# The order of the loads between an attention's end and the first half of an output projection

## Chip, core and metric

The kernel runs on one core of a Trainium2 chip. The metric is device time in microseconds (us) of one execution; lower is better. The engines are PE (TensorE, matrix products), ACT (ScalarE), DVE (VectorE), POOL (GpSimd) and SP (SyncE, which here issues every load and store). Each works through its own list of instructions in order and waits on semaphores for the others.

## The reference

One layer of a hybrid encoder on 1024 tokens of width 1024, with 16 meta tokens ahead of them, all in float32:

```python
h = concat([meta_tokens, x])                 # 1040 rows
u = rmsnorm(h, norm_mix)
a, q, k, v, r, lr, ga, gb = split(u @ w_in)
y_a = (multiscale_pool(a) grouped @ w_pool_mix * pool_scale) @ w_pool_out
o = chunked_gated_linear_attention(q, k, v, log_decay(lr @ w_gate_up + b_gate))   # chunks of 64
y_b = (rmsnorm(o, gla_norm) * silu(r)) @ w_gla_out
m = sigmoid(ga) * y_a + sigmoid(gb) * y_b
h = h + m @ w_out
h = h + square(relu(rmsnorm(h, norm_ffn) @ w_ff1)) @ w_ff2
out = rmsnorm(h, norm_final) without the meta rows
```

The change lies around `y_b`, `m` and `m @ w_out`.

## The kernel before

Float32 products are made of three fp32r matmuls (`mm3`): each operand is split into a high part (ACT copies it to fp32r) and a low part (the rest, a subtraction on DVE, or on POOL while the attention runs). So a block of weights goes through a load into a raw tile, the high part on ACT and the low part on DVE or POOL before PE can use it.

The tokens are worked on in two halves of 512, called half 0 and half 1. The attention (`gla`) has four units, two for each half; while it runs, filler work is poured between its steps: the projections for k, v and the gate gb, and then `yb_block(n, 0)`, the product with w_gla_out for half 0. `yb_block(n, h)` makes two products of 128 output columns each: 12 matmuls into a bank (L1044 and L1045 on DVE multiply it by the stored gate gb and add the stored y_a part, ACT copies the high part th at L1048, POOL makes the low part tl at L1049). Half 0 and half 1 have eight such products each. The gate tiles come from HBM in pairs, a tile of gb_dram (L992) and one of ma_dram (L993), by `yb_load`, into three buffers for each half (t and o); a buffer is free when POOL has made the tl of the product that used it.

The weights of w_gla_out come in four blocks of 512 KB through a ring of two (`Ring`): `top_up` loads the next block into a raw tile (L101) and splits it (L77 on ACT, L78 on DVE or POOL) as soon as a place in the ring is counted as done. Half 0 uses blocks 0 to 3, and keeps 2 and 3; half 1 uses 2 and 3 from the ring first, then loads 0 and 1 again (`YB`).

The output projection follows. w_out is loaded and split in two column halves of four blocks each (`load_wo(ch, kk)`, L1324 and L1325), of 512 KB. `out_tile(t, ch)` makes 128 tokens by 512 columns with 24 matmuls, and DVE adds the bank to x (L1357), which `x_again(t)` has loaded again into the tile `acc`. `acc` (eight tiles of 512 KB) lies where the attention's buffers were, so its pool opens when the last user of those buffers is done.

What sets the order: PE's list is in program order throughout (`tc.manual_schedule`). The lists of ACT and DVE are in program order from `early_gates` to `wo1_open`. The list of SP is made by a scheduler, which moves a load ahead of others when its place is free. `early_gates` stands in the code where the attention's last unit has been issued, in the middle of half 0's products.

Of the kernel before, what the change touches and what calls it, by code (L numbers as in the profile page):

```python
# [15 lines left out]
P = 128  # L16
D = 1024
# [3 lines left out]
HALF = 512  # L21
# [84 lines left out]
def kernel(  # L106
# [3 lines left out]
    nc = tc.nc  # L110
# [3 lines left out]
    w_gate_up, b_gate, gla_norm, w_gla_out, w_out = w_gate_up[0], b_gate[0], gla_norm[0], w_gla_out[0], w_out[0]  # L114
    norm_ffn, w_ff1, w_ff2 = norm_ffn[0], w_ff1[0], w_ff2[0]
# [8 lines left out]
    def banks(keep=0, **tags):  # L124
        while len(ps_open) > keep:
            ps_open.pop().__exit__(None, None, None)
            wide.pop(psp.popitem()[0], None)
        for tag, n in tags.items():
            cm = tc.tile_pool(name=f"ps_{tag}", bufs=n, space=bass.MemoryType.PSUM)
            psp[tag] = cm.__enter__()  # L130
            ps_open.append(cm)
# [31 lines left out]
    gB = left.push("gB", [P, D], F32)  # L163
# [16 lines left out]
    raw = Raw(nc, [left.push(f"raw{i}", [P, D], F32) for i in range(2)])  # L180
# [10 lines left out]
    def f32(ap):  # L191
        return ap.bitcast(F32)
# [4 lines left out]
    def bcast(v):  # L197
        return v[None, :].broadcast_to([P, D])
# [202 lines left out]
    S, rings = {}, [W1]  # L401

    def step(steps, fn, ring=None, aps=()):
        steps.append((ring, list(aps), fn))
# [29 lines left out]
    def buffer(key, depth, size=HALF):  # L434
        S[key] = left.push(key, [P, depth, size], F32)
        S["n" + key], S["d" + key] = 0, depth

    def nxt(key):
        i = S["n" + key]
        S["n" + key] += 1  # L440
        return S[key][:, i % S["d" + key]]
# [345 lines left out]
    one = []  # L787
# [122 lines left out]
    def rows4(w, j):  # L910
        return w[:, j * 256 : (j + 1) * 256].rearrange("(k p) c -> p k c", p=P)
# [74 lines left out]
    def yb_load(n, h):  # L986

        if n >= 8 or (n, h) in staged:
            return
        d = 2 * YB[h][n // 2] + n % 2  # L990
        gl, ml = staged[n, h] = (nxt("t2"), nxt("o2")) if h else (nxt("t1"), nxt("o"))
        nc.sync.dma_start(gl, gb_dram[d, h])  # L992
        nc.sync.dma_start(ml, ma_dram[d, h])  # L993

    def in_order(on):


        if on:
            S["order"] = tc.manual_schedule(engines={mybir.EngineType.Activation, mybir.EngineType.DVE})
            S["order"].__enter__()  # L1000
        else:
            S.pop("order").__exit__(None, None, None)

    def early_gates():

        in_order(True)
        left.pop_to(S["left_n"])
        for key in ("t2", "o2"):
            S[key] = right.push(key, [P, 3, HALF], F32)
            S["n" + key], S["d" + key] = 0, 3  # L1010
        S["raw3"] = right.push("raw3", [P, D], F32)
        for n in range(3):
            yb_load(n, 1)

    kept = {}

    def yb_block(n, h):
        j = YB[h][n]

        def fn(*wbs):  # L1020
            if h == 0 and n > 1:
                kept[j] = wbs[0]
            wb = wbs[0] if wbs else kept[j]
            hi, lo = (t.rearrange("p (k c) -> p k c", k=4) for t in wb)
            assert h or ("o", 0) in done
            yg = S["yg"][h]
            for e in range(2):
                d, w = 2 * j + e, slice(e * P, (e + 1) * P)
                for m in range(2 + h):
                    yb_load(2 * n + e + m, h)  # L1030
                gl, ml = staged[2 * n + e, h]
                b = bank("mm")
                for k in range(4):
                    mm3(
                        b, 1, lambda i: (hi[:, k, w], lo[:, k, w]),
                        lambda i: (yg[:, 0, k], yg[:, 1, k]), first=k == 0, last=k == 3,
                    )
                    yield 3 * 512 / 2400
                if e and not wbs:
                    W1.done, W1.kept = W1.done + 1, W1.kept - 1  # L1040
                    W1.top_up()
                elif e:
                    yield "keep" if j in kept else "free"
                dve.tensor_tensor(gl, b, gl, ALU.mult)  # L1044
                dve.tensor_tensor(gl, gl, ml, ALU.add)  # L1045
                th = MH[h][:, d]
                tl = ML[h][:, d]
                act.activation(th, gl, ACT.Copy)  # L1048
                pool.tensor_tensor(tl, gl, f32(th), ALU.subtract)  # L1049

        return fn
# [211 lines left out]
    def gla():  # L1263
# [16 lines left out]
        for n, u in enumerate(units + [None]):  # L1280
            if u is None:
                early_gates()
            live = side + old + ([inside(*u, units[n - 1] if n else None)] if u else [])
            while live:
                waits = [(g, next(g, None)) for g in live]
                live = [g for g, w in waits if w is not None]
                pour(max([w for _, w in waits if w is not None], default=0) * PACE)
                if not live:
                    break
            if n == 2:  # L1290
                done.add(("o", 0))
            if n == 0:
                while ("k", 1) not in done:
                    next(filler)
            old = [across(*u)] if u else []
            side = [meta_state(1)] if n == 0 else []
# [7 lines left out]
    def merge_open():  # L1304
        W1.eng = dve
        banks(keep=1, x=2, ms=4)
        rota["mm"] = ("mm", "mm", "x", "x")
        left.pop_to(base)
        S["wo"] = [left.push("wo0", [P, 2, KT, HALF], F32R)]
        S["left_acc"] = left.mark()  # L1310
        S["acc"] = left.push("acc", [P, 8, D], F32)
        raw.lend(S["raw3"])
        nc.sync.dma_start(gB, bcast(norm_ffn))

    def x_again(t):
        nc.sync.dma_start(S["acc"][:, t], x[t * P : (t + 1) * P, :])

    def load_wo(ch, kk):
        def fn():
            wo = S["wo"][ch][:, :, 2 * kk : 2 * kk + 2]  # L1320
            c = slice(ch * HALF, (ch + 1) * HALF)
            r = raw.load(w_out[kk * 256 : (kk + 1) * 256, c].rearrange("(k p) c -> p k c", p=P), D)
            r = r.rearrange("p (k c) -> p k c", k=2)
            act.activation(wo[:, 0], r, ACT.Copy)  # L1324
            dve.tensor_tensor(wo[:, 1], r, f32(wo[:, 0]), ALU.subtract)  # L1325

        return fn

    step(one, merge_open)
    def wo1_open():  # L1330
        in_order(False)
        raw.back()
        right.pop_to(0)
        buffer("u2", 2, D)
        S["u2p"] = right.push("u2p", [P, 2, HALF], F32)
        S["rawx0"] = right.push("rawx0", [P, D], F32)
        raw.lend(S["rawx0"])
        S["right_ff"] = right.mark()
        S["wo"].append(right.push("wo1", [P, 2, KT, HALF], F32R))
# [4 lines left out]
    def out_tile(t, ch):  # L1344
        def fn():
            half, at = t // 4, (t % 4) * P
            wo = S["wo"][ch]
            b, n = bank("mm"), ORDER.index(t)
            for j in range(2):
                if ch and j and n > 1:  # L1350
                    turn_tile(ORDER[n - 2])
                mm3(
                    b, KT // 2, lambda i: (MH[half][:, 4 * j + i, at : at + P], ML[half][:, 4 * j + i, at : at + P]),
                    lambda i: (wo[:, 0, 4 * j + i], wo[:, 1, 4 * j + i]), first=j == 0, last=j == 1,
                )
            a = S["acc"][:, t, ch * HALF : (ch + 1) * HALF]
            dve.tensor_tensor(a, b, a, ALU.add)  # L1357
            if ch:
                layer_norm(S["acc"][:, t], S["u2"][:, n % 2])
                nc.sync.dma_start(h_dram[t], S["acc"][:, t])  # L1360

        return fn
# [31 lines left out]
            dve.tensor_tensor(fl, a, f32(fh), ALU.subtract)  # L1394

    for n, j in enumerate(YB[1]):
        if n < 2:
            step(one, yb_block(n, 1))
        else:
            step(one, yb_block(n, 1), W1, [rows4(w_gla_out, j)])  # L1400
        if n:
            step(one, load_wo(0, n - 1))
    step(one, load_wo(0, 3))
    step(one, wo1_open)
    for t in range(8):
        step(one, lambda t=t: x_again(t))
        step(one, out_tile(t, 0))
        if 1 < t < 6:
            step(one, load_wo(1, t - 2))


    def first_blocks():
        ff_quarters.places = [raw.own, [S["rawx0"], None]]
        for i, u in ((0, 0), (0, 1), (1, 0)):
            ff_quarters.load(i, u)
# [262 lines left out]
```

## Time and profile before

| | us |
|---|---|
| three runs | 1247.72, 1245.71, 1245.96 |
| median | 1245.96 |
| span of the profiled execution | 1247.8 |

The page gives no time of the profiled execution beside its span; the span lies 0.1 us above the slowest of the three runs, so next to nothing lies around it.

| stretch of the profiled execution | from, us |
|---|---|
| first product with w_gla_out, half 0 | 466.0 |
| first output tile (m @ w_out) | 515.7 |
| second output tile | 531.4 |
| output tiles of w_out's second half end, squared-ReLU MLP follows | about 640 |

How to read it: PE is busy nearly throughout, so the places where PE waits are what a change in the order of loads can move. The views used below are the page, the waits of an engine, windows (busy time of each engine in a stretch, with the clock granted to PE and the share in which the DMA engines were busy) and the timeline of an engine. A row of a timeline has the start, the duration, the engine, the line, the operation, what is written and read, the count, and in brackets the idle time before it with what ended it.

### The profile page before, as it was taken

The numbers are of one execution on the slowest core, as the hardware profiler recorded it, in microseconds if no ns is written. First come the engines' busy times: TensorE is split into PE (matmuls) and PEld (weight loads), VectorE is DVE, ScalarE is ACT, GpSimd is POOL, SyncE is SP. The second block draws the span as 40 slices with busy tenths as digits, with TensorE's granted clock in tenths as the row PEclk, the third lists the DMA queues.
The fourth block names the chain that finished last, engine by engine and source line by source line (L and its number), as shares of the span: only waits on it lengthen the run. The fifth ranks groups of instructions, "written<-read, shape, count | busy, mean of one in ns | idle before, by whom it ended". The sixth has DMA issues, their size and how long they took to land.

```text
span 1247.8 us, 18255 instructions
## 1 busy us (share of the span) xinstructions
PE 1213.1 (97%) x6822; PEld 1006.5 (81%) x6822; DVE 850.7 (68%) x1384; ACT 615.4 (49%) x1092; POOL 65.0 (5%) x70
## 2 busy tenths in 40 slices
PE   7999999999999999799999999999999999999997
PEld 6878888988887788688878888888887788888886
DVE  6897676653556677723897676766774777887786
ACT  6667567321446663412654554555553444444554
POOL 2100000001101115300000000000000000000000
PEclk9999999999999999899999999999999999999999
DMA  8033326156102246831234544544569773333432
GB/s 249 2 109 104 109 85 197 52 161 204 36 19 61 86 140 223 284 104 51 94 117 155 167 152 136 164 156 135 177 219 371 267 247 94 102 93 100 162 96 90
DMA packets 142682, 173.85 MB, mean 139 GB/s; under 512 B 10969, under 2 KB 82417, under 8 KB 142593
## 3 DMA queue, kind: packets, MB, share of 16 engines
q1 hardware_dynamic: 142592, 172.68, 42.8%
q8 instruction: 54, 0.88, 0.3%
q14 instruction: 36, 0.29, 0.1%
HBM read 119.17 MB, written 53.48 MB: 138 GB/s over the span
## 4 chain that ended last, share of the span: by engine, by line
PE 90%; DVE 5%; DMA 2%; issue 1%; ACT 1%; SPq 0%; DVEq 0%; ACTq 0%
PE b_mm L246 11%; PE b_mm L247 11%; PE b_mm L248 11%; PE b_ms L246 9%; PE b_ms L247 9%; PE b_ms L248 9%; PE b_x L246 8%; PE b_x L248 8%; PE b_x L247 8%; PE b_sc L1128 1%; PE b_mx L246 1%; PE b_mx L247 1%; PE b_mx L248 1%; PE b_ms L538 1%; DMA raw<-hf_dram 1%
## 5 line engine op out<-in xcount | busy, mean ns | idle before, releaser
L246 PE MATMUL b_mm<-th,w1h 128*128 128x512 f32 (+1 forms) x312 | 117.8, 378 | 3.2 <-ACT th L1385 2.1
L247 PE MATMUL b_mm<-tl,w1h 128*128 128x512 f32 (+1 forms) x312 | 116.0, 372 | 0.6 <-DVE tl L1386 0.6
L248 PE MATMUL b_mm<-th,w1l 128*128 128x512 f32 (+1 forms) x312 | 115.8, 371 | 0.0
L246 PE MATMUL b_x<-th,w1h 128*128 128x512 f32 (+1 forms) x240 | 90.8, 378 | 0.0
L247 PE MATMUL b_x<-tl,w1h 128*128 128x512 f32 (+1 forms) x240 | 90.6, 378 | 0.0
L248 PE MATMUL b_x<-th,w1l 128*128 128x512 f32 (+1 forms) x240 | 90.3, 376 | 0.0
L264 ACT ACTIVATE w1h<-raw 128x512 fp32r<-128x512 f32 x96 | 59.6, 621 | 36.7 <-PE b_x L247 14.1
L265 DVE TENSOR_TENSOR w1l<-raw,w1h 128x512 fp32r<-128x512 f32 x96 | 65.6, 684 | 12.3 <-ACT w1h L264 12.3
L246 PEld LDWEIGHTS b_mm<-th,w1h 128*128 128x128 f32 x312 | 58.5, 188 | 16.5 <-issue 3.3
L264 ACT ACTIVATE w1h<-fs 128x512 fp32r<-128x512 f32 x72 | 45.4, 631 | 46.4 <-PE b_ms L247 31.7
L247 PEld LDWEIGHTS b_mm<-tl,w1h 128*128 128x128 f32 x312 | 58.6, 188 | 10.5 <-DVE tl L1386 0.9
L248 PEld LDWEIGHTS b_mm<-th,w1l 128*128 128x128 f32 x312 | 58.6, 188 | 10.3
L264 ACT ACTIVATE w1h<-bt 128x512 fp32r<-128x512 f32 x44 | 27.8, 632 | 67.7 <-issue 59.5
L265 DVE TENSOR_TENSOR w1l<-fs,w1h 128x512 fp32r<-128x512 f32 x72 | 49.3, 685 | 14.7 <-ACT w1h L264 14.6
L1535 DVE TENSOR_TENSOR bt<-w,w 128x512 f32<-128x512 f32 x80 | 54.6, 683 | 0.4 <-DMA w<-in_w_ff_dram 0.4
L248 PEld LDWEIGHTS b_x<-th,w1l 128*128 128x128 f32 x240 | 45.1, 188 | 8.5
L246 PEld LDWEIGHTS b_x<-th,w1h 128*128 128x128 f32 x240 | 45.0, 188 | 8.4
L247 PEld LDWEIGHTS b_x<-tl,w1h 128*128 128x128 f32 x240 | 45.1, 188 | 8.2
L264 ACT ACTIVATE fxh<-bt 128x512 fp32r<-128x512 f32 x36 | 22.8, 632 | 57.6 <-issue 48.1
L246 PE MATMUL b_ms<-wo,w1h 128*128 128x512 f32 x128 | 49.8, 389 | 0.0
L247 PE MATMUL b_ms<-wo,w1h 128*128 128x512 f32 x128 | 49.8, 389 | 0.0
L248 PE MATMUL b_ms<-wo,w1l 128*128 128x512 f32 x128 | 49.8, 389 | 0.0
(438 smaller groups left out, 3370.2 us busy)
## 6 DMA issues: line engine op xcount, KB each, us to landing
hf_dram<-h SPq DMA_DIRECT2D x112, 256.0 KB, 2.1
raw<-hf_dram SPq DMA_DIRECT2D x112, 256.0 KB, 2.6
w<-in_w_ff_dram SPq DMA_DIRECT2D x64, 256.0 KB, 4.8
raw<-in_w_in_dram SPq DMA_DIRECT2D x24, 512.0 KB, 4.8
raw<-in_w_ff_dram SPq DMA_DIRECT2D x16, 512.0 KB, 4.1
rawx<-in_w_ff_dram SPq DMA_DIRECT2D x16, 512.0 KB, 4.0
xs<-in_x_dram SPq DMA_DIRECT2D x8, 512.0 KB, 4.9
rawx<-in_w_in_dram SPq DMA_DIRECT2D x8, 512.0 KB, 4.4
```

Of the source, the lines that this page charges most:

```text
L246: pe.matmul(ps, ah, bh, start=first and i == 0, stop=False, skip_group_check=more)
L247: pe.matmul(ps, ah, bl, start=False, stop=False, skip_group_check=more)
L248: pe.matmul(ps, al, bh, start=False, stop=last and i == n - 1, skip_group_check=more)
L264: act.activation(hi, a, ACT.Copy)
L265: dve.tensor_tensor(lo, a, f32(hi), ALU.subtract)
L538: pe.transpose(b[j][:, i], u[:, (4 * j + i) * P : (4 * j + i + 1) * P], ident)
L1128: pe.matmul(b[to, e, j], kk[r, s], qq[r, s], start=True, stop=True, tile_position=(e * CH, u * CH))
L1535: dve.tensor_tensor(bt, w, S["w2"][q[3:]][:, i], ALU.add if q[2] == "+" else ALU.subtract)
```

## The change

- From `early_gates` to `first_blocks`, SP's list is in program order as well (`in_order` now takes a key and the engines).
- w_out's first half: block 0 is loaded in `early_gates` into the tile raw3, which took part in the rotation of raw tiles before; block 1 in `merge_open` into the idle tile `acc[:, 5]`; blocks 2 and 3 behind the first and the second `yb_block` of half 1, into `acc[:, 6]` and `acc[:, 7]`. The split of block n stands ahead of `yb_block(n, 1)` (before, that of block n - 1 stood behind it).
- norm_ffn (gB) is loaded behind half 1's products instead of in `merge_open`; x is loaded behind it, two tiles ahead of the output tiles.

```diff
-    def in_order(on):
-        if on:
-            S["order"] = tc.manual_schedule(engines={mybir.EngineType.Activation, mybir.EngineType.DVE})
-            S["order"].__enter__()
-        else:
-            S.pop("order").__exit__(None, None, None)
+    def in_order(key, *engines):
+        S[key] = tc.manual_schedule(engines=set(engines))
+        S[key].__enter__()
+
+    def any_order(key):
+        S.pop(key).__exit__(None, None, None)
 
     def early_gates():
-        in_order(True)
+        in_order("loads", mybir.EngineType.SP)
+        in_order("order", mybir.EngineType.Activation, mybir.EngineType.DVE)
...
         for n in range(3):
             yb_load(n, 1)
+        fetch_wo(0, 0, S["raw3"])
...
-        raw.lend(S["raw3"])
-        nc.sync.dma_start(gB, bcast(norm_ffn))
+        fetch_wo(0, 1, S["acc"][:, 5])
...
+    fetched = {}
+
+    def fetch_wo(ch, kk, at=None):
+        c, rows = slice(ch * HALF, (ch + 1) * HALF), w_out[kk * 256 : (kk + 1) * 256]
+        ap = rows[:, c].rearrange("(k p) c -> p k c", p=P)
+        if at is None:
+            at = raw.load(ap, D)
+        else:
+            nc.sync.dma_start(at.rearrange("p (k c) -> p k c", k=2), ap)
+        fetched[ch, kk] = at.rearrange("p (k c) -> p k c", k=2)
+
     def load_wo(ch, kk):
         def fn():
-            wo = S["wo"][ch][:, :, 2 * kk : 2 * kk + 2]
-            c = slice(ch * HALF, (ch + 1) * HALF)
-            r = raw.load(w_out[kk * 256 : (kk + 1) * 256, c].rearrange("(k p) c -> p k c", p=P), D)
-            r = r.rearrange("p (k c) -> p k c", k=2)
+            if (ch, kk) not in fetched:
+                fetch_wo(ch, kk)
+            wo, r = S["wo"][ch][:, :, 2 * kk : 2 * kk + 2], fetched.pop((ch, kk))
             act.activation(wo[:, 0], r, ACT.Copy)
             dve.tensor_tensor(wo[:, 1], r, f32(wo[:, 0]), ALU.subtract)
...
     for n, j in enumerate(YB[1]):
+        step(one, load_wo(0, n))
         if n < 2:
             step(one, yb_block(n, 1))
         else:
             step(one, yb_block(n, 1), W1, [rows4(w_gla_out, j)])
-        if n:
-            step(one, load_wo(0, n - 1))
-    step(one, load_wo(0, 3))
+        if n < 2:
+            step(one, lambda kk=n + 2: fetch_wo(0, kk, S["acc"][:, 4 + kk]))
+
+    def load_gB():
+        nc.sync.dma_start(gB, bcast(norm_ffn))
+
+    step(one, load_gB)
     step(one, wo1_open)
+    step(one, lambda: x_again(0))
+    step(one, lambda: x_again(1))
     for t in range(8):
-        step(one, lambda t=t: x_again(t))
+        if t < 6:
+            step(one, lambda t=t: x_again(t + 2))
         step(one, out_tile(t, 0))
...
     def first_blocks():
+        any_order("loads")
```

In the built program the list of SP from the attention's end on then reads (a pair is a gb tile and an ma tile): pairs for the first two products of half 0; three pairs for half 1, with a gb store among them; w_out block 0; pair; w_gla_out block 2; two pairs; w_gla_out block 3; pair; the r tile; two pairs; w_out block 1; pair; w_gla_out block 0 again; w_out block 2; two pairs; w_gla_out block 1 again; w_out block 3; two pairs; norm_ffn; x tiles, with w_out's second half between them. The list of PE is the same as before. On ACT and DVE only the w_out splits, and behind them the first splits of w_ff1, have other places.

More of the change, by code (lines that the diff above doesn't have):

```diff
@@ L1330, in wo1_open @@
     def wo1_open():
-        in_order(False)
+        any_order("order")
         raw.back()
```

## The prediction

> **What bounds the kernel now.** I read the page first, then the waits of TensorE around the change, then the windows and the timelines of the engines there.
>
> ```profile
> span 1247.8 us, 18255 instructions
> ...
> PE 1213.1 (97%) x6822; PEld 1006.5 (81%) x6822; DVE 850.7 (68%) x1384; ACT 615.4 (49%) x1092; POOL 65.0 (5%) x70
> ```
>
> TensorE (PE) is busy for 97% of the span, so a change in loads can gain only what PE loses around them. The waits of PE from 440 to 560 us:
>
> ```profile
> PE b_mm L246 <- ACT wo L1324: 4.6, 2, 4.1
> PE b_mm L247 <- DVE wo L1325: 2.0, 2, 1.3
> ```
>
> All the 6.6 us of waiting lie in the first output tile, which needs the split blocks of w_out. The windows (us; PE, PEld, DVE, ACT and POOL busy; granted clock; DMA share; GB/s) show a second cost behind them:
>
> ```profile
> 520.00:524.00 4.00, 1.01 (x5) 0.49 (x3) 3.17 (x4) 1.19 (x3) 1.26 (x1) 0.68 0.92 250
> 524.00:528.00 4.00, 2.24 (x4) 1.45 (x5) 2.95 (x3) 3.86 (x5) 1.27 (x1) 0.50 1.02 395
> ```
>
> The clock falls to 0.50 behind the 4.1 us wait. The timeline of PE gives the places in time that I count from:
>
> ```profile
> 480.89 0.40 PE L246 MATMUL b_mx<-yg,w1h 128*128 128x512 f32 x1
> ...
> 489.65 1.04 PE L1256 MATMUL b_m<-ident,mix 128*128 128x128 f32 x8
> ...
> 504.83 0.39 PE L246 MATMUL b_mm<-yg,w1h 128*128 128x512 f32 x1
> ...
> 510.27 0.39 PE L246 MATMUL b_x<-yg,w1h 128*128 128x512 f32 x1
> ...
> 515.71 0.39 PE L246 MATMUL b_mm<-wo,th 128*128 128x512 f32 x1
> ...
> 527.15 0.63 PE L248 MATMUL b_mm<-wo,tl 128*128 128x512 f32 x1
> ...
> 531.42 0.51 PE L246 MATMUL b_x<-wo,th 128*128 128x512 f32 x1
> ```
>
> I call the eight products of yb_block on half 0 A0 to A7 and those on half 1 B0 to B7; two of them share a block of w_gla_out. A4 starts at 480.89, the last transposes of the attention stand at 489.65 inside A6, B4 starts at 504.83, B6 at 510.27. These last two are 24 matmuls apart, so a matmul takes 0.227 us. Output tile 0 starts at 515.71 and tile 1 at 531.42. From 527.15 to 531.42 ten matmuls take 0.427 us each: twelve of them (from about 526.6) lost 12 x 0.2 = 2.4 us to the clock. What the change can gain at most is thus 6.6 + 2.4 = 9.0 us.
>
> **What is moved.** The in-order list of SP (the engine that issues every load) now is the order of the code. That brings w_out forward, but it takes four other loads back: the third and fourth w_gla_out block of half 0 (GA2, GA3) and the two that half 1 loads again (GB2, GB3). In the code a block is asked for where the ring tops up, behind the gate loads of the product before (yb_load). Before, the scheduler had taken them far ahead:
>
> ```profile
> 453.36 0.38 SPq L101 DMA_DIRECT2D raw<-in_w_gla_out_dram  x1
> ...
> 468.82 0.38 SPq L101 DMA_DIRECT2D raw<-in_w_gla_out_dram  x1
> 469.54 0.32 SPq L977 DMA_DIRECT2D gb_dram<-o  x1
> ...
> 475.74 0.97 SPq L101 DMA_DIRECT2D raw<-in_w_gla_out_dram  x2
> ```
>
> GA2 was issued at 453.36, GA3 at 468.82, and GB2 and GB3 together at 475.74, 29 us ahead of B4. In the changed list GA2 stands behind the gate pair for A2, whose second load waits until the gb store issued at 469.54 has landed; GA3 stands behind the pair for A4, which reuses the buffer of A1; GB2 behind the pair for B3 (buffer of B0); GB3 behind the pair for B5 (buffer of B2). Such a buffer is free when GpSimd has done its tl. SP really stops there, with all that is queued behind:
>
> ```profile
> SPq L992 <- POOL tl L1049: 17.7, 10, 3.3
> ```
>
> So each block now waits for the end of a product's evacuation (DVE L1044 and L1045, ACT th, POOL tl), and the next evacuations on DVE and ACT are queued behind the block's own split (L77, L78). That is a loop of load, split, evacuation, load.
>
> **The terms.** Rows of ACT, POOL and DVE:
>
> ```profile
> 481.06 1.04 ACT L77 ACTIVATE w1h<-raw 128x1024 fp32r<-128x1024 f32 x1
> ...
> 483.64 1.00 ACT L1247 ACTIVATE mix<-b_m 128x1024 f32<-128x1024 f32 x1
> ...
> 497.65 0.63 ACT L1048 ACTIVATE th<-t 128x512 fp32r<-128x512 f32 x1 [0.69 <-DVE t L1045]
> ...
> 510.87 1.04 ACT L1324 ACTIVATE wo<-raw 128x1024 fp32r<-128x1024 f32 x1
> ...
> 473.20 2.40 POOL L78 TENSOR_TENSOR w1l<-raw,w1h 128x1024 fp32r<-128x1024 f32 x1 [0.71 <-ACT w1h L77]
> ...
> 478.04 1.26 POOL L1049 TENSOR_TENSOR tl<-t,th 128x512 fp32r<-128x512 f32 x1 [2.43 <-ACT th L1048]
> ...
> 497.04 4.71 POOL L1049 TENSOR_TENSOR tl<-t,th 128x512 fp32r<-128x512 f32 x3 [3.15 <-ACT th L1048]
> ...
> 487.60 1.22 DVE L1252 TENSOR_TENSOR mix<-b_m,small 128x1024 f32<-128x1024 f32 x1
> ...
> 493.73 1.23 DVE L1260 TENSOR_TENSOR yg<-mix,yg 128x1024 fp32r<-128x1024 f32 x1 [1.13 <-ACT yg L1259]
> 494.89 0.68 DVE L1044 TENSOR_TENSOR t<-b_mm,t 128x512 f32<-128x512 f32 x1
> ...
> 497.54 0.68 DVE L1044 TENSOR_TENSOR t<-b_mm,t 128x512 f32<-128x512 f32 x1
> ...
> 500.98 1.85 DVE L78 TENSOR_TENSOR w1l<-raw,w1h 128x1024 fp32r<-128x1024 f32 x1 [1.65 <-ACT w1h L77]
> ...
> 511.94 1.47 DVE L1325 TENSOR_TENSOR wo<-raw,wo 128x1024 fp32r<-128x1024 f32 x1 [1.65 <-ACT wo L1324]
> ...
> 528.70 1.21 DVE L1325 TENSOR_TENSOR wo<-rawx,wo 128x1024 fp32r<-128x1024 f32 x1
> ```
>
> From 494.89 to 497.54 two products (A6, A7) are evacuated, so one costs DVE 1.33 us. A split's high part costs ACT 1.04, its low part POOL 2.40 (half 0), or DVE between 1.21 and 1.85 (half 1: I take 1.5). An issue on SP is 0.4. The times to landing, from the page and from small windows of the issues (KB, us to landing):
>
> ```profile
> gb_dram<-o SPq DMA_DIRECT2D x16, 256.0 KB, 2.8
> ...
> raw<-in_w_gla_out_dram SPq DMA_DIRECT2D x6, 512.0 KB, 4.6
> ...
> raw<-in_w_gla_out_dram SPq DMA_DIRECT2D x1, 512.0 KB, 3.9
> ...
> gb_dram<-o SPq DMA_DIRECT2D x1, 256.0 KB, 5.3
> ...
> raw<-in_w_gla_out_dram SPq DMA_DIRECT2D x2, 512.0 KB, 7.3
> ```
>
> 3.9 is GA2's own at 453, with the queue nearly free; 5.3 is the store at 469.54 behind other loads; 7.3 the pair at 475.74. I take 4.6 for each block, and 2.8 and 5.3 as the two ends for the store, written "early / late" below.
>
> **Step 1, GA2 and GA3.** The store lands at 472.3 / 474.8. GA2 is issued 0.4 later and lands at 477.3 / 479.8; its high part is done at 478.4 / 480.9, the low part on POOL at 480.8 / 483.2. A4 starts at 480.89 and reads the low part with its third matmul, 0.46 later, so this alone costs PE 0 / 1.9. A1's tl is next on POOL: 482.0 / 484.5. The gate pair for A4 (0.8), and GA3 is issued at 482.8 / 485.3, lands at 487.4 / 489.9, high part at 488.5 / 491.0. On ACT the copy th of A3 (0.63) and then the attention's last Square (L1247) stand behind it: L1247 ends at 490.1 / 492.6, where before it ended at 484.64. It is 5.4 / 7.9 late, and DVE's chain from it to yg had no gap worth counting: L1252 ended 0.8 before the transposes used it. The transposes are 4.6 / 7.1 late, and the low part of yg, before done at 494.96, is done at 500.4 / 502.9.
>
> **Step 2, GB2.** DVE evacuates A6 and A7 (2.65), ACT makes A7's th (0.63), then comes what the change puts here: the first w_out split, 1.04 on ACT and 1.47 on DVE. B0's evacuation (1.33, th 0.63, tl 1.26) follows: 509.4 / 511.9. Its gate pair takes 0.8, GB2 is issued at 510.2 / 512.7, lands at 514.8 / 517.3, is split at 517.3 / 519.8. PE could begin B4 at 504.83 + 4.6 / 7.1 = 509.4 / 511.9, and waits over 6 us.
>
> **Step 3, GB3.** B1's evacuation was queued behind that split: 1.33, th 0.63; the second w_out split 1.04 and 1.47; B2's evacuation 1.33, th 0.63, tl 1.26: 525.0 / 527.5. With 0.8, GB3 is issued at 525.8 / 528.3, lands at 530.4 / 532.9, is split at 532.9 / 535.4. PE then has 22 matmuls of B6 and B7 (5.0) and the 24 of output tile 0 (5.4): tile 1 starts at 543.4 / 545.9 instead of 531.42, **12.0 / 14.5 us late**.
>
> **Step 4, the clock.** In front of B6 PE has been idle for over 5 us, longer than the 4.1 us that took the clock to 0.50. I add the 2.4 us worked out above; the cold stretch after B4's wait costs nothing, since PE then waits for GB3 anyway. The Trainium skill (TensorE: Matmul & The Clock Gate, Part 1) has the clock halved after an idle window of about 3.4 us and released after as long a busy one; by that the loss is an estimated 1.7 us and the sum 0.7 us less. The trace had the longer half-rate stretch, and the row decides.
>
> **What costs nothing.** The 6.6 us wait for w_out goes: the blocks 0 to 2 are in SBUF long before tile 0; the last one's split stands behind the evacuation of B5 on DVE, about 10 us after GB3's split, when tile 0 reaches it: 0 to 0.7 us. x lands after tile 0, but its add (L1357) only empties a bank, and there are four banks, or 16 us, of cover. norm_ffn is first read eight output tiles, or 44 us, later. Were that cover gone, x would cost a load's landing, some 4.6 us.
>
> **Sum.** 12.0 + 2.4 = 14.4 early, 14.5 + 2.4 = 16.9 late; I take 15.5, between them, as the store has fewer loads ahead of it than before but not none. The four landings are 3.9 at best (-2.8) and, by the single crowded row, 5.3 (+2.8): from 12.0 + 2.4 - 2.8, or 9.2 with a clock that stays up, to 16.9 + 2.8 + 0.7 = 20.4. The sum is made in the profiled execution (span 1247.8, the runs shown 1245.71 to 1247.72) and put on the median of 1245.96: **1261.5 us**, own range 1255 to 1266.4.
>
> **Rivals.** (a) *Faster, the change does what its words say*: w_out is there in time, PE waits for nothing, all 9.0 us come back: 1237. It holds if GB2 and GB3 are split by 504.8 and 510.3, which needs their issue about 7 us before (landing, both parts of the split); it turns at the point where B0's tl ends before 497. For it speaks that 6.6 us are really lost to w_out now. The Trainium skill (DMA: Bandwidth & Descriptors, Rules for kernel authors) says to issue a load early and wait late, which is this rival for w_out; it is as much against the change for w_gla_out. Against it: B0 starts only after A7, and its tl, the third of the POOL row at 497.04, ended at 501.8 already in the trace of before. Chance 0.09. (b) *The attention's end is not touched*: GA3 comes soon enough that L1247 isn't delayed, and only steps 2 to 4 count: 14.4 - 5.4 = 9.0, or 1255. For it: a store that lands at once and a free queue; against it: A1's tl ended at 479.3 even before, so GA3 is issued after 480 at best. Chance 0.10. (c) *Crowded landings*: two to four blocks take 7.3 us, +5.4 to +10.8: 1267 to 1272. Against it: far fewer bytes are now in flight when the blocks are asked for. Chance 0.09. My forecast has 0.71.
>
> **Range and chances.** 1252 to 1268 leaves out (a), half of (c) and the ends of the forecast, not over 0.2. About 0.2%, 2.5 us, is what a measurement of this kernel can tell from none. Faster 0.09 is (a); no change would need the loss to meet the 9.0 us of (a), 0.01; slower, all the rest, 0.90.
>
> **What would show it.** Right: w_gla_out issues at about 473, 483, 511 and 526; PE waits for ACT or POOL w1h/w1l (L77, L78) at A6, B4 and B6, 6 us and more at the last two; no wait for wo over 1 us; tile 1 at about 545; a low clock behind B4 and B6. Wrong: no PE wait for L77 in half 1, or B4 at 505. If the blocks are late but the sum is off, the landings are what I mis-sized.

## The result, and the profile after

| | before | after |
|---|---|---|
| median of four runs, us | 1246.04 | 1266.32 |
| lowest to highest | 1245.71 to 1247.72 | 1265.56 to 1269.84 |

The change costs 20.3 us: the ratio is 1.0164, with a 95% interval of 1.0147 to 1.018. The forecast was 1261.5 us, 15.5 us slower than before, with a range that ends at 1268. The profiled execution took 1266.35 us, 1.85 us more than its span. In every run below the difference is 1.7 to 1.9 us too, so the execution profiled before, with a span of 1247.8 us, took about 1249.6 us (an estimate), which is more than its runs; more lies around a span than was said above.

```profile
span 1264.5 us, 18250 instructions
...
PE 1216.4 (96%) x6822; PEld 1006.9 (80%) x6822; DVE 850.1 (67%) x1384; ACT 615.7 (49%) x1092; POOL 64.3 (5%) x70
```

No engine has more work than before: the counts are the same, and PE's busy time is only 3.3 us longer. What grew is idle time, so the next view is the waits of PE from 440 to 580 us (engine, line, what it waited for: us in total, times, longest):

```profile
PE b_mm L246 <- ACT w1h L77: 9.2, 2, 6.8
PE b_x L246 <- ACT w1h L77: 8.5, 1, 8.5
PE b_mm L248 <- POOL w1l L78: 1.7, 1, 1.7
PE b_mx L248 <- POOL w1l L78: 1.7, 1, 1.7
```

The waits for w_out (L1324 and L1325 before) are gone, all 6.6 us of them. In their place stand 21.1 us of waits for the split of a w_gla_out block. The waits of SP's queue from 440 to 560 us say why those blocks come late:

```profile
SPq L992 <- POOL tl L1051: 55.8, 8, 10.8
```

L992 is the load of a gate tile. It stood for 17.7 us before; now SP stands at such loads for 55.8 us, in program order, and every load behind them stands too. SP's timeline gives the issues (start, duration, line, what is loaded):

```profile
468.45 0.32 SPq L977 DMA_DIRECT2D gb_dram<-o  x1
469.29 0.46 SPq L1328 DMA_DIRECT2D raw<-in_w_out_dram  x1
...
472.23 0.39 SPq L101 DMA_DIRECT2D raw<-in_w_gla_out_dram  x1
...
485.31 0.43 SPq L101 DMA_DIRECT2D raw<-in_w_gla_out_dram  x1
...
512.95 0.32 SPq L992 DMA_DIRECT2D t<-gb_dram  x1
...
513.79 0.43 SPq L101 DMA_DIRECT2D raw<-in_w_gla_out_dram  x1
514.26 0.51 SPq L1328 DMA_DIRECT2D acc<-in_w_out_dram  x1
...
530.22 0.43 SPq L101 DMA_DIRECT2D raw<-in_w_gla_out_dram  x1
530.70 0.51 SPq L1328 DMA_DIRECT2D acc<-in_w_out_dram  x1
```

The four L101 rows are GA2, GA3, GB2 and GB3. They were issued at 453.36, 468.82 and, both of half 1, 475.74 before: they are now 19, 16, 38 and 54 us later. Right behind GB2 and GB3 the changed kernel asks for w_out blocks 2 and 3 (L1328), and 2.9 us ahead of GA2 for block 0.

The view of the DMA issues, in a small window around each of the four (KB, us to landing), in the same order:

```profile
raw<-in_w_gla_out_dram SPq DMA_DIRECT2D x1, 512.0 KB, 6.6
...
raw<-in_w_gla_out_dram SPq DMA_DIRECT2D x1, 512.0 KB, 4.9
...
raw<-in_w_gla_out_dram SPq DMA_DIRECT2D x1, 512.0 KB, 5.4
...
raw<-in_w_gla_out_dram SPq DMA_DIRECT2D x1, 512.0 KB, 6.1
```

All four lie over the 4.6 us that the prediction took.

PE's timeline has the waits at their places (in brackets the idle time before the row), and the two output tiles:

```profile
482.53 0.49 PE L248 MATMUL b_mx<-yg,w1l 128*128 128x512 f32 x1 [1.70 <-POOL w1l L78]
...
491.41 0.50 PE L246 MATMUL b_mm<-yg,w1h 128*128 128x512 f32 x1 [2.37 <-ACT w1h L77]
...
520.37 0.79 PE L246 MATMUL b_mm<-yg,w1h 128*128 128x512 f32 x1 [6.83 <-ACT w1h L77]
...
537.55 0.79 PE L246 MATMUL b_x<-yg,w1h 128*128 128x512 f32 x1 [8.47 <-ACT w1h L77]
...
539.41 0.63 PE L246 MATMUL b_x<-yg,w1h 128*128 128x512 f32 x1
...
543.25 0.47 PE L246 MATMUL b_mm<-yg,w1h 128*128 128x512 f32 x1
...
546.07 0.39 PE L246 MATMUL b_mm<-wo,th 128*128 128x512 f32 x1
...
551.51 0.39 PE L246 MATMUL b_x<-wo,th 128*128 128x512 f32 x1
```

The bracketed rows are A4, A6, B4 and B6; two rows, inside B6 and at the head of B7, follow, which step 4 below uses, then tile 0 and tile 1. Tile 1 starts at 551.51 instead of 531.42. The first w_gla_out product starts at 464.9 instead of 466.0, so the stretch between them grew by 20.1 + 1.1 = 21.2 us. That is the result within 1 us. The rest of the two executions isn't alike: it took 1.1 us less ahead of the stretch and 3.4 us less behind it, so the span grew by 16.7 us only. Over all the kernels here the part behind the start of tile 1 takes 712 to 717 us, and the execution before, with 716, lies near the top. That nothing outside the stretch matters is therefore argued, not shown. Within the stretch the waits grew by 21.1 - 6.6 = 14.5 us; the rest is for the most part PE at a lower clock, which step 4 below comes back to.

In the experiments "shift" is this same growth of the stretch, read from each kernel's trace, and each ratio is to runs of the kernel before made beside it (medians of 1246.57 or 1247.35 us), so ratios compare better than times.

### The profile page after: what moved, and what is told of

Same layout as the page of the kernel before. It is cut to its first block, busy times and chain, and to the rows that moved or that the text cites. A ratio compares the mean times of both kernels' runs of the same rounds, so it can differ in the third digit from the quotient of the medians.

```text
span 1264.5 us, 18250 instructions
## 1 busy us (share of the span) xinstructions
PE 1216.4 (96%) x6822; PEld 1006.9 (80%) x6822; DVE 850.1 (67%) x1384; ACT 615.7 (49%) x1092; POOL 64.3 (5%) x70
## 4 chain that ended last, share of the span: by engine, by line
PE 87%; DVE 5%; DMA 4%; ACT 2%; issue 1%; POOL 1%; SPq 0%; ACTq 0%; DVEq 0%
PE b_mm L246 11%; PE b_mm L247 10%; PE b_mm L248 10%; PE b_ms L246 9%; PE b_ms L247 9%; PE b_ms L248 9%; PE b_x L248 8%; PE b_x L246 8%; PE b_x L247 8%; DMA raw<-in_w_gla_out_dram 2%; PE b_sc L1130 1%; PE b_mx L246 1%; PE b_mx L247 1%; PE b_mx L248 1%; DMA hf_dram<-h 1%
## 5 line engine op out<-in xcount | busy, mean ns | idle before, releaser
L246 PE MATMUL b_mm<-th,w1h 128*128 128x512 f32 (+1 forms) x312 | 117.8, 378 | 1.9 <-DVE c L749 1.1
L246 PE MATMUL b_x<-th,w1h 128*128 128x512 f32 (+1 forms) x240 | 90.8, 378 | 0.0
L246 PEld LDWEIGHTS b_mm<-th,w1h 128*128 128x128 f32 x312 | 58.5, 188 | 15.1 <-issue 3.2
L264 ACT ACTIVATE w1h<-bt 128x512 fp32r<-128x512 f32 x44 | 27.8, 632 | 66.9 <-issue 58.0
L77 ACT ACTIVATE w1h<-raw 128x1024 fp32r<-128x1024 f32 x22 | 23.3, 1057 | 74.3 <-DMA raw<-in_w_gla_out_dram 33.8
L246 PEld LDWEIGHTS b_x<-th,w1h 128*128 128x128 f32 x240 | 45.0, 188 | 8.5
L246 PE MATMUL b_ms<-wo,w1h 128*128 128x512 f32 x128 | 49.8, 389 | 0.0
```

What stands on the lines that cost most here:

```text
L77: self.nc.scalar.activation(hi, raw, ACT.Copy)
L246: pe.matmul(ps, ah, bh, start=first and i == 0, stop=False, skip_group_check=more)
L264: act.activation(hi, a, ACT.Copy)
```

## The experiments

**Theory 1** is the prediction's: the order of SP's list holds four w_gla_out blocks behind gate loads, and nothing else in the change costs. **Theory 2** (its rival (c), and any like it): the loads are slow because of their company, or the w_out splits between the evacuations cost, so that the new tiles and places do part of the harm.

**The tiles without the order.** The change as it is, but SP's list is left to the scheduler:

```diff
 def early_gates():
-    in_order("loads", mybir.EngineType.SP)
...
 def first_blocks():
-    any_order("loads")
```

> The change without SP's program order: the w_out blocks still go into raw3 and the idle tiles of acc and are still split ahead of each product, but the scheduler orders the loads again. Theory (the in-order list takes the w_gla_out blocks back, and that is the whole loss): the waits for w1h (L77, L78) in half 1 fall from 15 us to under 5, the wait for w_out is gone, and the time is below before: 1240 to 1243. It doesn't reach 1237, because the first two w_out splits now stand ahead of the evacuations of B0 and B2 on DVE, and hold up the split that B6 needs by some 4 us. Rival (the splits ahead of the products, not the order of the loads, are what is late): 1255 or more, with the same waits at B4 and B6.

Measured: 1240.98 us, ratio 0.9961 (0.995 to 0.9971); shift -5.4 us. Faster than before, as theory 1 has it. PE's waits in the same stretch:

```profile
PE b_x L246 <- ACT w1h L77: 2.0, 1, 2.0
PE b_x L248 <- DVE w1l L78: 0.8, 1, 0.8
```

The idle tiles and the earlier splits bring what they were made for; one order on one engine turns that into a loss.

**The order without the tiles.** The kernel before, with SP's list in program order over the same stretch:

```diff
     def in_order(on):
         if on:
+            S["loads"] = tc.manual_schedule(engines={mybir.EngineType.SP})
+            S["loads"].__enter__()
...
     def first_blocks():
+        S.pop("loads").__exit__(None, None, None)
```

> The kernel before with SP in program order from early_gates to first_blocks, and nothing else. Theory: the same loop of load, split, evacuation, load for GA3, GB2 and GB3, a little shorter (no w_out split in it), and the w_out blocks then come later than before, behind the last gate pairs: tile 1 at 548 to 553, time 1263 to 1270. Rival (the new places of w_out are the cause): 1246, as before.

Measured: 1280.51 us, ratio 1.0273 (1.0256 to 1.0289); shift +29.0 us. The direction was right, the size over 10 us too small: the late w_out blocks were expected, but with tile 1 at 548 to 553, and it starts at 560.12. Of the 33.9 us by which the time is longer, 4.9 lie outside the stretch and are not explained here. SP's timeline has the late blocks, and PE's timeline the price:

```profile
523.00 0.43 SPq L101 DMA_DIRECT2D raw<-in_w_gla_out_dram  x1
523.48 0.51 SPq L101 DMA_DIRECT2D raw<-in_w_out_dram  x1
...
540.77 1.46 SPq L101 DMA_DIRECT2D raw<-in_w_out_dram  x3
```

```profile
547.92 0.79 PE L246 MATMUL b_mm<-wo,th 128*128 128x512 f32 x1 [8.39 <-ACT wo L1326]
...
560.12 0.63 PE L246 MATMUL b_x<-wo,th 128*128 128x512 f32 x1
```

Without tiles of their own, w_out's blocks are themselves asked for in program order: three of them at 540.77, behind the last gate pair. Tile 0 waits 8.4 us for them and runs at half clock (0.50 granted). So the order costs w_gla_out in both kernels, and here w_out as well.

**The order kept, the four blocks asked for early.** The ring may load ahead of its split (`ask`), and the split stays where it was:

```diff
+    def ask(self):
+        ap = self.queue[self.loaded + len(self.asked)]
+        self.asked.append(self.raw.load(ap, ap.shape[1] * ap.shape[2]))
...
-            raw = self.raw.load(ap, n)
+            raw = self.asked.pop(0) if self.asked else self.raw.load(ap, n)
...
 def early_gates():
+    W1.ask()                        # GA2, ahead of half 1's gate pairs
...
+    W1.ask()                        # GA3, behind them
     fetch_wo(0, 0, S["raw3"])
...
+    W1.ask()                        # GB2 and GB3, at the head of merge_open
+    W1.ask()
```

> The change with SP in program order, but the raw loads of the w_gla_out blocks are asked for ahead of their split: GA2 at the head of early_gates, GA3 behind the three gate pairs there, GB2 and GB3 at the head of merge_open. Theory: both waits in half 0 go, B4 waits under 1 us and B6 some 4 us (the split behind w_out's on DVE): 1240 to 1244. Rival (in-order SP costs by the gate pairs themselves, whoever is behind them): 1255 or more.

Measured: 1240.1 us, ratio 0.9947 (0.9924 to 0.997); shift -5.6 us. PE's waits (four lines further down in this kernel: L250 is L246):

```profile
PE b_x L250 <- ACT w1h L81: 2.0, 1, 2.0
PE b_x L252 <- DVE w1l L82: 0.7, 1, 0.7
```

Program order is no loss by itself: with these four loads ahead of the gate loads that SP stands at, 18.4 of the 21.1 us of waits for w_gla_out are gone, and what is left (2.0 + 0.7) is what the free order leaves too (2.0 + 0.8). SP itself still stands at gate loads (L996 is L992) for longer than the 17.7 us of before:

```profile
SPq L996 <- POOL tl L1057: 31.7, 9, 5.2
```

So it isn't SP's standing that costs, but what stands behind it.

**One half's blocks at a time.** The same edit with only the first two `ask` lines (GA2, GA3), and with only the last two (GB2, GB3):

> The change, with only GA2 and GA3 asked for ahead of their split (as in w_gla_out_asked_early); GB2 and GB3 stay where the change has them. Theory (two delays that add up, since DVE's chain from the attention's last Square to the evacuation of B2 has no slack): the 9.5 us by which yg's low part came late go, the waits at B4 and B6 stay at about 7 and 8.5 us: 1255 to 1259. Rival (half 1's own loop starts from the gate pairs and absorbs the delay of half 0): 1262 or more.

> The change, with only GB2 and GB3 asked for at the head of merge_open; GA2 and GA3 stay late. Theory of two delays that add up: the waits in half 0 stay (some 6 us in three places), B4 waits under 1 us and B6 some 3 us: 1248 to 1251, and the gains of this run and of the one with GA2 and GA3 early add up to the 26 us between the changed kernel and w_gla_out_asked_early. Rival (slack in half 1): 1241 to 1244.

Measured: 1257.21 us, ratio 1.0087 (1.0065 to 1.0108), shift +10.1 us, and 1250.86 us, ratio 1.0026 (1.0013 to 1.0039), shift +4.5 us. PE's waits, first with half 0's blocks early, then with half 1's:

```profile
PE b_x L250 <- ACT w1h L81: 7.6, 1, 7.6
PE b_mm L250 <- ACT w1h L81: 6.7, 1, 6.7
```

```profile
PE b_mm L250 <- ACT w1h L81: 2.7, 1, 2.7
PE b_x L250 <- ACT w1h L81: 2.1, 1, 2.1
...
PE b_mx L252 <- POOL w1l L82: 1.6, 1, 1.6
```

The first kernel keeps the waits of B4 and B6 and loses those of A4 and A6; the second the other way round, but for the 2.9 us at B6 that all four early blocks leave too. By the ratios, half 0's blocks are worth 1.0164 - 1.0087 = 0.0077 and half 1's 1.0164 - 1.0026 = 0.0138, together 0.0215; asking for all four early gave 1.0164 - 0.9947 = 0.0217. Within the intervals, some 0.002 each, the two halves add up; by the shifts they bring 11.1 + 16.7 = 27.8 us, and all four blocks 26.8. For rival (b), the attention's end is really delayed: the first kernel puts that and GA2's own waits at 0.0077 x 1246 = 9.6 us.

**What makes the blocks land late: w_out ahead of the gates.** w_out blocks 1 to 3 all asked for in `merge_open`:

```diff
-        fetch_wo(0, 1, S["acc"][:, 5])
+        for kk in (1, 2, 3):
+            fetch_wo(0, kk, S["acc"][:, 4 + kk])
...
-        if n < 2:
-            step(one, lambda kk=n + 2: fetch_wo(0, kk, S["acc"][:, 4 + kk]))
```

> The change with w_out's blocks 1, 2 and 3 all asked for in merge_open, so that no 512 KB load stands right behind GB2 and GB3. Landing theory 1 (the load behind shares the DMA engines with the block): GB2 and GB3 land in 4.6 us or less instead of 5.4 and 6.2, time 1263 to 1265. Landing theory 2 (a block behind a gate pair takes that long anyway): 5.2 to 6.2 as in the changed kernel, time 1265 to 1268.

Measured: 1268.71 us, a single run, inconclusive: one load had nothing behind it and landed in 4.7 us (GB3), another had three loads of 512 KB ahead of it and took 5.9 us up to its split (GB2). The shift is +19.7 us, 1.5 less than in the change, while the one time is 2.4 us longer, so the time decides nothing.

**Nothing right behind the blocks.** w_out blocks 2 and 3 asked for inside `yb_block(n, 1)`, one gate pair later (11 us behind GB2 and GB3 in the trace), so that no load stands close behind them:

```diff
+                if h and not e and n in (1, 2):
+                    fetch_wo(0, n + 1, S["acc"][:, 5 + n])
...
-        if n < 2:
-            step(one, lambda kk=n + 2: fetch_wo(0, kk, S["acc"][:, 4 + kk]))
```

> The change, with w_out's blocks 2 and 3 asked for four to five microseconds later (behind the gate pairs of B4 and B6), so that nothing is issued right behind GB2 and GB3; all else as in the change. Theory of the landings (a 512 KB load issued within half a microsecond behind a block lengthens its landing): GB2 and GB3 land in 4.6 to 4.9 us instead of 5.4 and 6.1, time 2 us lower: 1263.5 to 1265. Rival (the pair ahead makes the landing long): landings of 5.2 to 6.2, time 1266.

Measured: 1265.49 us, ratio 1.0148 (1.0134 to 1.0162); shift +18.6 us. The DMA issues of GB2 and GB3 in this kernel (KB, us to landing), where the change had 5.4 and 6.1:

```profile
raw<-in_w_gla_out_dram SPq DMA_DIRECT2D x1, 512.0 KB, 4.9
...
raw<-in_w_gla_out_dram SPq DMA_DIRECT2D x1, 512.0 KB, 4.8
```

The landings are 0.5 and 1.3 us shorter with nothing behind them, and the wait at B6 falls from 8.5 to 7.6 us. The shift is 2.5 us smaller; the two ratios' intervals overlap, so the landings show the effect and the total time, 0.5 us above the expected range, alone would not. Theory 2 thus has a small share.

**A version that beats both kernels.** The blocks asked for early, and the low parts of w_out blocks 0 and 1 made on POOL, which has little to do then:

```diff
-            dve.tensor_tensor(wo[:, 1], r, f32(wo[:, 0]), ALU.subtract)
+            (pool if ch == 0 and kk < 2 else dve).tensor_tensor(wo[:, 1], r, f32(wo[:, 0]), ALU.subtract)
```

> w_gla_out_asked_early, with the low parts of w_out's blocks 0 and 1 made on POOL instead of DVE. Theory (what is left of the wait at B6, 2.7 us, is DVE's queue: the two w_out low parts ahead of B0's and B2's evacuation): the wait at B6 goes, 1237 to 1238.5. Rival (POOL at 2.4 us each holds back the tl of B0 to B3 and with it the gate pairs, or slows DVE by sharing): 1240 or more, with waits at B3 to B5 for gate tiles.

Measured: 1238.78 us, ratio 0.9932 (0.9918 to 0.9945); shift -7.9 us. The time is 0.3 us above the expected range. PE's waits left in the stretch:

```profile
PE b_mm L251 <- DVE wo L1345: 0.9, 1, 0.9
PE b_x L252 <- DVE w1l L82: 0.5, 1, 0.5
```

The wait at B6 falls from 2.7 to 0.5 us, so most of it was DVE's queue with the w_out low parts in it; a wait of 0.9 us for a w_out low part is new. It is the fastest of all here, though its interval overlaps with that of the version with the blocks asked for early alone. It takes 7.9 of the at most 9.0 us that the prediction worked out for this stretch.

## Why the prediction was right, and by how much it was off

The direction and the mechanism were right, the size was 4.8 us short (15.5 forecast, 20.3 measured). The positions below stand as predicted, early / late, less the 1.1 us by which this execution is ahead of the one before:

| point | predicted, us | measured, us |
|---|---|---|
| GA2 issued | 471.6 / 474.1 | 472.23 |
| GA3 issued | 481.7 / 484.2 | 485.31 |
| last Square ends | 489.0 / 491.5 | 492.78 |
| low part of yg done | 499.3 / 501.8 | 503.41 |
| GB2 issued | 509.1 / 511.6 | 513.79 |
| GB3 issued | 524.7 / 527.2 | 530.22 |
| tile 1 starts, clock included | 544.7 / 547.2 | 551.51 |

The measured column starts between the ends, is 1.1 us past the late one at GA3, 2.2 at GB2, 3.0 at GB3 and 4.3 at tile 1: no link of the chain is missing, one term that recurs is too small.

**Step 1** held in kind. The store landed in 3.4 us (issued 468.45, the pair's load that waits for it at 471.82), between 2.8 and 5.3 and near the early end. A4 waited 1.7 us, within 0 / 1.9. The chain over the last Square was right, and rows of ACT and DVE show it: GA3's split, the Square (L1249 in this kernel), yg's low part.

```profile
490.30 1.06 ACT L77 ACTIVATE w1h<-raw 128x1024 fp32r<-128x1024 f32 x1 [9.22 <-DMA raw<-in_w_gla_out_dram]
...
491.78 1.00 ACT L1249 ACTIVATE mix<-b_m 128x1024 f32<-128x1024 f32 x1
```

```profile
502.17 1.24 DVE L1262 TENSOR_TENSOR yg<-mix,yg 128x1024 fp32r<-128x1024 f32 x1 [1.13 <-ACT yg L1261]
...
507.71 1.85 DVE L1337 TENSOR_TENSOR wo<-raw,wo 128x1024 fp32r<-128x1024 f32 x1 [1.65 <-ACT wo L1336]
```

**Steps 2 and 3** held: B4 and B6 wait 6.83 and 8.47 us, "6 us and more". The first w_out split that the change puts ahead of B0's evacuation took DVE 1.85 us (L1337 above) instead of 1.47, 0.4 us of the miss.

**The mis-sized term: the four landings.** I took 4.6 us for each, the median of six in the trace of before, so 18.4 in all; they took 6.6 + 4.9 + 5.4 + 6.1 = 23.0. That is 4.6 us of the 5.7 by which the shift of 21.2 us exceeds the forecast's 15.5. For GB2 and GB3 their company in the queue sets it, as the experiment above shows, and the change itself put it there; for GA2 and GA3 that is argued:

| block of 512 KB | what stands beside it | landing, us |
|---|---|---|
| GA2: order without the tiles | no w_out block near | 3.9 |
| GA2: the change; nothing behind; half 1's blocks early; w_out ahead of the gates | w_out block 0 asked for 2.5 to 3.0 us ahead | 6.6; 6.0; 6.6; 6.0 |
| GA3: the change; nothing behind; order without the tiles; w_out ahead of the gates; half 1's blocks early | a gate pair and the r tile behind, in all five | 4.9; 4.9; 5.5; 5.8; 5.2 |
| GA3: half 0's blocks early; all four early; low parts on POOL | asked for 15 to 16 us sooner than in the change, w_out block 0 0.5 us behind | 5.2; 5.6; 5.9 |
| GB2 and GB3: nothing behind | no w_out block near | 4.9, 4.8 |
| GB2: order without the tiles; GB3: w_out ahead of the gates | no w_out block near | 4.7; 4.7 |
| GB2 and GB3: the change; half 0's blocks early | a w_out block 0.5 us behind | 5.4, 6.1; 5.7, 5.6 |
| GB3: order without the tiles | a w_out block 0.5 us behind | 6.2 |

For GB2 and GB3 the four values without a w_out block and the five with one don't overlap. GA3, with the same neighbours in five kernels, spreads by 0.9 us, and the three with a w_out block behind it lie in much the same range (5.2 to 5.9): a part of its excess is spread. For GA2 the cause is a comparison of kernels that differ in more than w_out block 0, not a test of that one load. I had the crowded row of 7.3 us before me and kept it for rival (c), with the reason that far fewer bytes are in flight. That reason is the weak step: the new w_out loads are issued next to three of the four blocks. The 23.0 us also lie above what the upper end of the prediction's own range allowed (four landings of 5.3, 21.2 us). That 1266.32 still lies within that range, 0.1 us below its end of 1266.4, is partly luck: that end takes the store at its late value, and it landed near the early one.

The other 1.1 us is the net of small terms: +1.0 between GA2's landing and GA3's issue (6.5 us, where 5.5 was predicted), +0.8 beside the landing between GA3's issue and GB2's (the w_out split on DVE added 0.4 and slower transposes, see step 4, 0.9; other steps took some off) and -0.6 (the store, against the middle of its two ends).

**Step 4** held for B4 and B6, and left out a third place, at A6. The windows (us; PE, PEld, DVE, ACT and POOL busy; granted clock; DMA share; GB/s) show the clock behind the waits at A6 and behind both long waits:

```profile
492.00:496.00 4.00, 2.30 (x6) 1.77 (x6) 2.87 (x6) 1.30 (x3) 3.02 (x2) 0.52 0.01 4
...
520.00:524.00 4.00, 3.59 (x8) 2.39 (x9) 2.52 (x3) 1.38 (x3) 0.36 (x1) 0.50 0.00 1
...
536.00:540.00 4.00, 2.41 (x5) 1.49 (x6) 2.43 (x3) 1.06 (x1) 0.00 (x0) 0.50 0.03 11
540.00:544.00 4.00, 4.00 (x12) 3.11 (x11) 2.32 (x4) 1.57 (x2) 1.29 (x1) 0.58 0.20 33
```

At A6 PE waited twice, 2.37 us for the high part and 1.70 for the low part with two matmuls between, and the clock fell to 0.52 there too. The attention's last transposes stand in that stretch and took 1.90 us instead of 1.04:

```profile
497.31 1.90 PE L1258 MATMUL b_m<-ident,mix 128*128 128x128 f32 x8
```

In PE's timeline above the nine matmuls from 539.41 to 543.25 stand 0.427 us apart, as in the trace of before, and then the pace is warm. The 24 matmuls from B6 at 537.55 to tile 0 at 546.07 took 8.5 us where 24 x 0.227 = 5.4 would be warm: 3.1 us, of which 12 x 0.2 = 2.4 is the clock, as forecast, and 0.7 lies almost wholly in the first three, where PE waits for the low part, which the prediction had counted with the split. The estimate from the Trainium skill (TensorE: Matmul & The Clock Gate, Part 1), 1.7 us, was the lower one; the 2.4 us of the trace differ from it by 0.7.

**What was to cost nothing** cost nothing: no wait for w_out, x or norm_ffn is left in the stretch.

**The rivals.** (a) failed: its condition, GB2 and GB3 split by 504.8 and 510.3, was missed by over 15 and 27 us (B4 and B6 start at 520.37 and 537.55). The experiments with early blocks and with a free order came close to it, at 1240 and 1241. (b) failed: the last Square ended 8.1 us later than before (492.78 against 484.64), and removing this together with A4's wait brought 9.6 us. (c) has its share in the size: the landings were crowded, if not to 7.3 us.

## What to carry to other kernels

When a load is brought forward by fixing the order of an issuing engine, list what that order takes back: every load behind one that waits for a buffer waits too, here 55.8 us of such waiting in 120 us, and the loads that PE needs soonest must stand ahead of the first such wait. Ask for a block apart from its split, so that the load's place in the list isn't bound to the place of the work that reads it. And when loads are brought together, take their landing time from rows with the company that they will have, not from a median.

## What the runs showed of the hardware

In the runs on GB2 and GB3 a load asked for later lengthened the landing of one asked for earlier on the same queue. Behind a gate pair of 2 x 256 KB, 512 KB took 4.7 to 4.9 us with nothing close behind, and 5.4 to 6.2 us with another 512 KB issued 0.5 us behind; a w_out block asked for alone (at 508 us in the changed kernel) took 3.7 us. For GA3, with other loads ahead, the runs don't tell the two cases apart. The Trainium skill (DMA: Bandwidth & Descriptors, Two DMAs through the same engine are not ordered) says that the descriptors of one queue of one DMA engine start in order but are pipelined, and that nothing orders transfers across the 16 engines. The traces agree so far as the earlier load lands later with another right behind it; how the packets of the two mix was not read from them.
